# The sums' low products ahead of the others in pieces with an adding transfer, and the fourth group with two direct pieces

## The chip, the core and the metric

The kernel runs on one core of a Trainium2 chip. The metric is the device time of one execution in microseconds (us); three runs of the kernel before gave 2460.9, 2458.1 and 2459.9, with a median of 2459.9. Four engines work side by side: TensorE (PE) multiplies matrices, VectorE (DVE) and ScalarE (ACT) work on elements, GpSimd (POOL) here mostly issues transfers, and SyncE (SP) issues the loads. Each engine runs its instructions in the order in which the program issues them.

## The reference

One encoder block on 256 tokens of width 2048, all in fp32. It is framed by two gated feed-forward parts (FFN1 and FFN2), with a recurrent mixing part and a cross attention between them:

```python
def swiglu(h, w_up, w_down):
    gate, up = jnp.split(h @ w_up, 2, axis=-1)
    return (jax.nn.silu(gate) * up) @ w_down
...
x = x + 0.5 * swiglu(rms_norm(x, ffn1_norm), ffn1_w_up, ffn1_w_down)
...   # gated linear recurrence (HGRN2), RG-LRU, their merge
x = x + cross_attention(rms_norm(x, xattn_norm), rms_norm(mem, mem_norm), wq, wkv, wo)
x = x + 0.5 * swiglu(rms_norm(x, ffn2_norm), ffn2_w_up, ffn2_w_down)
return rms_norm(x, final_norm)
```

`w_up` is 2048 x 11264 and `w_down` 5632 x 2048. The change touches only the products with `w_up` in the two FFNs, how their weights are prepared, and the place of a few additions for FFN1's input.

## The kernel before, in words

**Products of two parts.** An fp32 product is made of three matmuls on a reduced format (fp32r): high x high, low x high and high x low. So each weight tile (128 x 2048, 1 MB, `raw`) is split into `h`, a copy by ACT into the reduced format, and `l = raw - h`, a subtraction on DVE (`split`, lines 117 to 121). The activations are split likewise into `xh` and `xl`. Helper `three` (line 455) issues for a list of products first the matmuls with the high part of the weights, two for each product (lines 458 and 459), and after them the matmuls with the low part, one for each (line 461). Low products therefore always come last in a piece, and PE needs `l` later than `h`.

**Groups and pieces.** Each FFN runs over 11 groups of 512 hidden columns with their gates (counted from 0 in the code, so that g = 3 is the fourth). A group has eight pieces p, one for each pair of 128-row blocks of the 2048 inputs. `ffn_order` (from line 42) writes the order of pieces out by hand, with blocks of the down product between the groups. A piece is done in one of three ways (`PRODUCTS`, lines 467 to 472; an entry names the activations' combination, the weights' combination and the accumulator):

- "plain" has 8 products, 24 matmuls, and uses the weights as they are (group 0 only).
- "fast" is a scheme of Strassen's kind with 7 products, 21 matmuls. Its first three products use parts of the weights themselves (`h` and `l`), its last four use sums of weights: `td` is made by three additions or subtractions on DVE (lines 217 to 219) and split into `th` (ACT, row L120) and `tl` (DVE, row L121), 1024 columns at a time.
- "mixed" has 8 products and 24 matmuls into the accumulators of the fast scheme. It combines activations, and needs the weights alone, no sums of them. Its weights are split as in "plain".

All matmuls of these pieces multiply a 128 x 128 activation block by a 128 x 512 part of the weights. From the fourth group on the pieces come in the order 1, 3, 4, 0, 2, 5, 6, 7, then four down blocks of 24 matmuls each; piece 0 is "mixed", the other seven "fast".

**Adding transfers.** To relieve DVE, the low part of some tiles is made without it: ACT copies the negated raw weights, rounded to the reduced format, into `l`, and a transfer issued by POOL adds the weights to it from memory. `plan_ffn` (line 130) says which tile takes which way. "fast added" (pieces 3, 4, 5 and 6 from the fourth group on) copies 1536 columns at line 224 and issues a 768 KB transfer at line 225; the copy `h` (line 226) follows. "added" (some down blocks) does it for a whole tile of 1 MB in `begin_added` (lines 190 to 197), with `h` made later at line 204. POOL's transfers go through one queue in order; the raw loads go through SP's.

**What sets the order.** `weights` (line 169) prepares tiles two pieces ahead of their use, in the order of the plan; an "added" tile's load, copy and transfer are issued one piece earlier still (line 177). The tile framework places waits and gives out buffers: three each for `raw`, for `h` and `th`, for `l`, and three shared by `td`, `tl` and the group's result `ev`; eight PSUM banks. A buffer of `l` is free again when the last matmul that reads it is done. Functions hung on a plan index (`rest`, `late_sums`, line 608) issue DVE's additions for FFN1's activation sums: for q = 1, 2, 3 at the indices 16, 17 and 18, behind the last subtraction issued.

Of the kernel before, what the change touches and what calls it, by code (L numbers as in the profile page):

```python
# [41 lines left out]
def ffn_order():  # L42

    out, down = [("plain", 0, p) for p in range(8)], [("down", 0, 1, c, 0) for c in range(4)]
    for g in range(1, NG):
        if g < 3:  # L50
            out += [(("mixed", "fast")[p % 2], g, p) for p in (0, 1, 2, 3, 5, 4, 7, 6)]
        else:
            out += [("fast" if p else "mixed", g, p) for p in (1, 3, 4, 0, 2, 5, 6, 7)]
        if g > 2 and g % 2:
            down = [("down", g - 2, 2, c, b) for c in range(4) for b in (g - 2, g - 1)]
        n = 2 if g < 3 else 4
        out, down = out + down[:n], down[n:]
    return out + [("down", NG - 2, 2, c, b) for c in range(4) for b in (NG - 2, NG - 1)]


@with_exitstack
def block_kernel(ctx: ExitStack, tc: tile.TileContext, xT, xin, memT, vec, gfin, bgate, lruw, wu1, wd1, win, wv,
# [30 lines left out]
    def bank(name="acc"):  # L93
        return psum.tile([P, 512], F32, name=name, tag="acc")
# [35 lines left out]
    def plan_ffn(name, wu, wd):  # L130
        for e in orders[name]:
            src = wd[e[4], e[3]] if e[0] == "down" else wu[e[1], e[2]]
            kind = "fast" if e[0] == "fast" else "plain"
            if e[0] == "down" and 0 < e[4] < NG - 1 and e[4] % 2 == 0 and e[3] % 2:
                kind = "added"
            if e[0] == "fast" and e[1] > 2 and e[2] in (3, 4, 5, 6):
                kind = "fast added"
            plan.append(((name,) + e, src, kind))

# [29 lines left out]
    def weights(*key):  # L169
        while plan and len(ahead) < 2:  # L170
            i = next(planned)
            k, src, kind = plan.pop(0)
            if i == 0:
                in_turn.enter_context(tc.manual_schedule(engines={sp.engine, act.engine, dve.engine}))
            if i < len(head):
                head[i]()
            if plan and plan[0][2] == "added":
                begun.append(begin_added(plan[0][1]))
            ahead.append((k, prepare(src, kind, 4 if i < 4 else 1)))
            if i in rest:  # L180
                rest[i]()
            if i == 7:
                in_turn.close()
        k, w = ahead.pop(0)
        assert k == key, (k, key)
        return w
# [79 lines left out]
    def flush(late):  # L266
        while late:
            late.pop(0)()
# [183 lines left out]

        return sums

    def three(products):

        for acc, (ah, al), (bh, bl), start, _ in products:
            pe.matmul(acc, ah, bh, start=start, stop=False)  # L458
            pe.matmul(acc, al, bh, start=False, stop=False)  # L459
        for acc, (ah, al), (bh, bl), _, stop in products:  # L460
            pe.matmul(acc, ah, bl, start=False, stop=stop)  # L461

    def part(pair, i, n):
        return [v[:, i * n:(i + 1) * n] for v in pair]
# [9 lines left out]
    def ffn(name, pairs, sq, then, begin=(), sums=()):  # L474
# [12 lines left out]
        def activate(sg, gate, up, t):  # L487

            act.activation(sg, gate, ACT.Silu, scale=rstd[:, t:t + 1])
            dve.scalar_tensor_tensor(out=sg, in0=up, scalar=rstd[:, t:t + 1], in1=sg, op0=ALU.mult, op1=ALU.mult)  # L490

        def turn(g, hid):
            for y in range(2):
                acc = bank()
                for z in range(2):
                    for t in range(2):
                        pe.transpose(acc[:, z * T + t * P:][:, :P], hid[t][:, (2 * y + z) * P:][:, :P], ident)  # L497
                o = slot(F32R, "hidop")
                ov = o.rearrange("p (z s c) -> p z s c", z=2, s=2)
                av = acc.rearrange("p (z c) -> p z c", z=2)  # L500
                act.activation(ov[:, :, 0], av, ACT.Copy)
                dve.tensor_tensor(out=ov[:, :, 1], in0=av, in1=ov[:, :, 0].bitcast(F32), op=ALU.subtract)
                hids[2 * g + y] = o
# [9 lines left out]
        for at, e in enumerate(order):  # L513
            w = weights(name, *e)
            kind = e[0]
            following = order[at + 1][0] if at + 1 < len(order) else None
            if kind != "down":
                g, p = e[1:]
                fast = kind == "fast"
                products = []  # L520
                for i, (a, b, n) in enumerate(PRODUCTS[kind]):
                    u = uses[g, n]
                    if u[0] == (p, i):
                        accs[n] = bank()
                    own, less = pairs[p]
                    products.append((accs[n], part(own, a, P) if a >= 0 else part(less, -1 - a, P), part(w[b // 4] if fast else w, b % 4, 512),
                                     u[0] == (p, i), u[-1] == (p, i)))
                three(products)
                last = at + 1 == len(order) or order[at + 1][1] != g or following == "down"
                ends = kind != "plain" and uses[g, 0][-1][0] == p  # L530
                if ends or last:
                    if ends or kind == "plain":
                        ev = scoped["wide"].tile([P, 2048], F32, name="ev", tag="wide")
                        e0, e1, e2, e3 = (ev[:, i * 512:(i + 1) * 512] for i in range(4))
                        if rstd is None:
                            with tc.issue_after(done["high"]):
                                rstd = sq.rstd_tokens()
                if ends:
                    act.activation(e0, accs[0], ACT.Copy)
                    dve.tensor_tensor(out=e1, in0=accs[5], in1=e0, op=ALU.add)  # L540
                    dve.tensor_tensor(out=e2, in0=accs[4], in1=e1, op=ALU.add)
                if last:
                    if kind == "plain":
                        activate(e0, accs[0], accs[1], 0)
                        activate(e3, accs[3], accs[2], 1)
                    else:
                        for o, n, x in ((e0, 1, e0), (e1, 3, e1), (e1, 2, e1)):
                            dve.tensor_tensor(out=o, in0=accs[n], in1=x, op=ALU.add)
                        activate(e0, e0, e1, 0)
                        for o, n, x in ((e3, 6, e2), (e2, 3, e2)):  # L550
                            dve.tensor_tensor(out=o, in0=accs[n], in1=x, op=ALU.add)
                        activate(e3, e3, e2, 1)
                    late.append((4 if g else 2, lambda g=g, hid=(e0, e3): turn(g, hid)))
            else:
                first, n, c, block = e[1:]
                if block == first:
                    accs["down"] = [bank(), bank()]
                for t in range(2):
                    products = []
                    for k in range(4):  # L560
                        a = hids[2 * block + k // 2][:, k % 2 * 512:][:, :512]
                        products.append((accs["down"][t], (a[:, t * P:][:, :P], a[:, T + t * P:][:, :P]),
                                         part(w, k, 512), block == first and k == 0, block == first + n - 1 and k == 3))
                    three(products)
                    if block == first + n - 1:
                        o = xt[c][:, t * 512:(t + 1) * 512]
                        done["residual"] = dve.scalar_tensor_tensor(out=o, in0=accs["down"][t], scalar=0.5, in1=o,
                                                                    op0=ALU.mult, op1=ALU.add).ins
                        if block == NG - 1:
                            then(c, t)  # L570
            if sums and not begin:
                sums.pop(0)()
            flush(begin)
            tick()
# [33 lines left out]
    def late_sums(q):  # L608
        with tc.issue_after(done["low"]):
            sums1[q](((0, "sums"),))  # L610

    for q, i in ((1, 16), (2, 17), (3, 18)):
        rest[i] = lambda q=q: late_sums(q)


# [49 lines left out]
    with scope(**FFN_POOLS):  # L665
        ffn("ffn1", pairs1, sq1, to_mix)
# [313 lines left out]
    for m in range(KT):  # L980
        acc = product(xs3.tiles, weights("q", m), late)
# [12 lines left out]
    for m in range(KT):  # L994
        acc = product(ms.tiles, weights("k", m))
# [53 lines left out]
    for h in range(HEADS):  # L1049
        for j in range(4):  # L1050
            acc = bank()
# [144 lines left out]
```

## Time and profile before

| | |
|---|---|
| median of three runs | 2459.9 us |
| the profiled execution's own time | 2457.71 us |
| its span | 2455.6 us |
| PE busy | 2427.0 us, 99% |
| DVE busy | 1883.5 us, 77% |
| ACT busy | 1486.4 us, 61% |
| POOL busy | 70.1 us, 3% |
| read from memory | 539.18 MB, 220 GB/s over the span |
| adding transfers of up weights | 64 of 768 KB |
| adding transfers of down weights | 16 of 1 MB |

The span is the stretch from the first to the last recorded instruction; the time of an execution has about 2 us more around it. In the profile's rows "L461 PE MATMUL acc<-l,xh" is a matmul issued at line 461, writing `acc` and reading `l` and `xh`. A number in square brackets or after the last bar is the engine's idle time just before, and the arrow names what it waited for. FFN1 lies between 0 and about 720 us, its fourth group at about 165 to 207 us; FFN2 lies between about 1750 us and the end, its fourth group at about 1900 to 1942 us.

### The profile page before, as it was taken

To read this page: it belongs to the slowest core of one execution; us is meant where nothing else is said; L and a number is where in the kernel's file an instruction comes from. 1 tells how busy PE (TensorE), PEld (TensorE's weight loads), DVE (VectorE), ACT (ScalarE), POOL (GpSimd) and SP (SyncE) were. 2 spreads that over 40 slices of the span, in tenths; PEclk is the share of its full clock that TensorE was granted. 3 is DMA by queue.
4 is the path that set the end of the run, shared out by engine and by line. 5 is a ranking of instruction groups with operands and counts; after the bars stand their busy time and mean duration, and the time that the engine had idled before them with its cause. 6 is when DMAs were issued, how large, how long until landed. Compare 5 with 4: busy or idle time off the path is not lost.

```text
span 2455.6 us, 30385 instructions
## 1 busy us (share of the span) xinstructions
PE 2427.0 (99%) x12202; PEld 2025.3 (82%) x12202; DVE 1883.5 (77%) x2057; ACT 1486.4 (61%) x1481; POOL 70.1 (3%) x84
## 2 busy tenths in 40 slices
PE   9999999999999999999999999999999999999998
PEld 8877888878788888888888888888888888887887
DVE  7998999989765757567665676556689999998985
ACT  8566677677564444477434554455555677776774
POOL 0000000000000000000000000000000000000000
PEclk9999999999999999999999999999999999999999
DMA  7578898989855544446554655444555989998894
GB/s 295 188 224 267 272 265 268 274 272 266 256 174 192 184 172 177 176 159 229 193 189 182 213 199 189 172 171 154 186 191 180 285 272 274 271 274 259 264 267 155
DMA packets 82220, 543.24 MB, mean 221 GB/s; under 512 B 9120, under 2 KB 9376, under 8 KB 24224
## 3 DMA queue, kind: packets, MB, share of 16 engines
q1 hardware_dynamic: 69840, 473.06, 52.5%
q0 software_dynamic: 11520, 67.11, 14.7%
q8 instruction: 95, 1.56, 0.2%
q10 hardware_dynamic: 720, 1.13, 0.1%
q14 instruction: 45, 0.37, 0.0%
HBM read 539.18 MB, written 2.10 MB: 220 GB/s over the span
## 4 chain that ended last, share of the span: by engine, by line
PE 88%; DMA 9%; ACT 1%; DVE 1%; issue 1%; ACTq 0%; SPq 0%; DVEq 0%
PE acc L461 16%; PE acc L458 14%; PE acc L459 14%; PE acc L240 11%; DMA l<-wu 8%; PE acc L261 8%; PE acc L262 8%; PE acc L264 8%; PE acc L244 5%; ACT l L224 1%; PE acc L497 1%; DMA raw<-wu 1%; PE acc L398 1%; ACT h L120 0%; PE acc L773 0%
## 5 line engine op out<-in xcount | busy, mean ns | idle before, releaser
L121 DVE TENSOR_TENSOR l<-raw,h 128x2048 fp32r<-128x2048 f32 (+2 forms) x372 | 790.0, 2128 | 337.0 <-ACT h L120 335.4
L120 ACT ACTIVATE h<-raw 128x2048 fp32r<-128x2048 f32 (+2 forms) x372 | 662.0, 1784 | 471.3 <-PE acc L262 205.7
L458 PE MATMUL acc<-h,xh 128*128 128x512 f32 x1256 | 490.6, 391 | 0.8 <-ACT h L120 0.8
L459 PE MATMUL acc<-h,xl 128*128 128x512 f32 x1256 | 488.9, 390 | 0.0
L120 ACT ACTIVATE h<-td 128x1024 fp32r<-128x1024 f32 x256 | 266.0, 1057 | 180.2 <-PE acc L459 88.8
L121 DVE TENSOR_TENSOR tl<-td,h 128x1024 fp32r<-128x1024 f32 x256 | 308.5, 1221 | 68.5 <-ACT h L120 66.9
L261 PE MATMUL acc<-h,ops 128*128 128x512 f32 x832 | 326.9, 393 | 0.0
L262 PE MATMUL acc<-h,ops 128*128 128x512 f32 x832 | 324.3, 390 | 0.0
L458 PEld LDWEIGHTS acc<-h,xh 128*128 128x128 f32 x1256 | 236.3, 188 | 51.7 <-ACT h L120 2.3
L240 PE MATMUL acc<-ops,h 128*128 128x512 f32 x1152 | 278.0, 393 | 0.3
L459 PEld LDWEIGHTS acc<-h,xl 128*128 128x128 f32 x1256 | 236.3, 188 | 49.0
L458 PE MATMUL acc<-h,hidop 128*128 128x512 f32 x704 | 275.7, 392 | 0.0
L459 PE MATMUL acc<-h,hidop 128*128 128x512 f32 x704 | 274.3, 390 | 0.0
L240 PEld LDWEIGHTS acc<-ops,h 128*128 128x128 f32 x1152 | 211.9, 188 | 42.9 <-DVE ops L301 0.9
L461 PE MATMUL acc<-l,xh 128*128 128x512 f32 x744 | 202.6, 394 | 17.7 <-DMA l<-wu 17.7
L264 PE MATMUL acc<-l,ops 128*128 128x512 f32 x832 | 206.1, 390 | 0.0
L461 PE MATMUL acc<-l,hidop 128*128 128x512 f32 x704 | 188.3, 389 | 0.0
L264 PEld LDWEIGHTS acc<-l,ops 128*128 128x128 f32 x832 | 156.2, 188 | 32.4
L261 PEld LDWEIGHTS acc<-h,ops 128*128 128x128 f32 x832 | 156.2, 188 | 32.3
L461 PEld LDWEIGHTS acc<-l,xh 128*128 128x128 f32 x744 | 138.2, 188 | 54.1 <-DMA l<-wu 26.7
L262 PEld LDWEIGHTS acc<-h,ops 128*128 128x128 f32 x832 | 156.3, 188 | 31.6
L217 DVE TENSOR_TENSOR td<-raw 128x1024 f32<-128x1024 f32 x128 | 155.9, 1218 | 6.1 <-DMA raw<-wu 3.9
(221 smaller groups left out, 2598.7 us busy)
## 6 DMA issues: line engine op xcount, KB each, us to landing
raw<-wu SPq DMA_DIRECT2D x172, 1024.0 KB, 6.1
raw<-wd SPq DMA_DIRECT2D x88, 1024.0 KB, 5.7
l<-wu POOLq DMA_DIRECT2D x64, 768.0 KB, 9.7
raw<-win SPq DMA_DIRECT2D x40, 1024.0 KB, 4.8
raw<-wg SPq DMA_DIRECT2D x32, 1024.0 KB, 4.8
l<-wd POOLq DMA_DIRECT2D x16, 1024.0 KB, 10.7
raw<-wab SPq DMA_DIRECT2D x16, 1024.0 KB, 4.8
raw<-wout SPq DMA_DIRECT2D x16, 1024.0 KB, 4.8
```

Of the source, the lines that this page charges most:

```text
L120: done["high"] = act.activation(h, raw, ACT.Copy).ins
L121: done["low"] = dve.tensor_tensor(out=l, in0=raw, in1=h.bitcast(F32), op=ALU.subtract).ins
L217: dve.tensor_tensor(out=two[0], in0=raw[:, None, :512].broadcast_to([P, 2, 512]), in1=two[1], op=ALU.subtract)
L224: act.activation(l[:, 512:], raw[:, 512:], ACT.Copy, scale=-1.0)
L240: pe.matmul(acc, h[:, k * P:(k + 1) * P], xs[k], start=k == 0, stop=False)
L244: done["product"] = pe.matmul(acc[:, :T], l[:, k * P:(k + 1) * P], xs[k][:, :T], start=False, stop=k == KT - 1).ins
L261: pe.matmul(accs[t], x[:, t * P:][:, :P], h[j], start=first and j == 0, stop=False)
L262: pe.matmul(accs[t], x[:, T + t * P:][:, :P], h[j], start=False, stop=False)
L264: done["product"] = pe.matmul(accs[t], x[:, t * P:][:, :P], l[j], start=False, stop=last and j == 3).ins
L458: pe.matmul(acc, ah, bh, start=start, stop=False)
L459: pe.matmul(acc, al, bh, start=False, stop=False)
L461: pe.matmul(acc, ah, bl, start=False, stop=stop)
```

## The change

It has two parts.

**The order of low products.** In fast pieces with an adding transfer, `three` now issues the low products of the sums (`tl`, products 3 to 6, four matmuls) ahead of those of the weights themselves (`l`, products 0 to 2, three matmuls). A function `adds` names these pieces: 3, 4, 5 and 6, from the fifth group on.

**The fourth group** (g = 3, in both FFNs). Its order becomes 1, 3, 0, 4, 2, 6, 5, 7. Piece 6 is "mixed" like piece 0, 24 matmuls for 21. Both mixed pieces take the way "added", a whole-tile adding transfer begun a piece earlier; the six fast pieces make `l` on DVE, so that this group has two adding transfers of 1 MB for four of 768 KB. Since piece 6 doesn't need the activation sums of the last quarter before the fifth group, the additions for q = 3 move from plan index 18 to 26.

```diff
         else:
-            out += [("fast" if p else "mixed", g, p) for p in (1, 3, 4, 0, 2, 5, 6, 7)]
+            out += [("mixed" if p == 0 or g == 3 and p == 6 else "fast", g, p)
+                    for p in ((1, 3, 0, 4, 2, 6, 5, 7) if g == 3 else (1, 3, 4, 0, 2, 5, 6, 7))]
...
+def adds(e):
+
+    return e[0] == "fast" and e[1] > 3 and e[2] in (3, 4, 5, 6)
...
-            kind = "fast" if e[0] == "fast" else "plain"
+            kind = "fast" if e[0] == "fast" else "added" if e[:2] == ("mixed", 3) else "plain"
             if e[0] == "down" and 0 < e[4] < NG - 1 and e[4] % 2 == 0 and e[3] % 2:
                 kind = "added"
-            if e[0] == "fast" and e[1] > 2 and e[2] in (3, 4, 5, 6):
+            if adds(e):
                 kind = "fast added"
...
-    def three(products):
+    def three(products, last=0):
+
 
         for acc, (ah, al), (bh, bl), start, _ in products:
             pe.matmul(acc, ah, bh, start=start, stop=False)
             pe.matmul(acc, al, bh, start=False, stop=False)
-        for acc, (ah, al), (bh, bl), _, stop in products:
+        for acc, (ah, al), (bh, bl), _, stop in products[last:] + products[:last]:
             pe.matmul(acc, ah, bl, start=False, stop=stop)
...
-                three(products)
+                three(products, 3 if adds(e) else 0)
...
-    for q, i in ((1, 16), (2, 17), (3, 18)):
+    for q, i in ((1, 16), (2, 17), (3, 26)):
         rest[i] = lambda q=q: late_sums(q)
```

## The prediction

> **What bounds the kernel now.** I read the page's busy table first, then its costliest groups, then the waits of TensorE (PE) by stretch, the order of time around single waits, and at last the chain behind one of them. The page, with columns of groups "busy, mean ns of one | idle before, releaser":
>
> ```profile
> span 2455.6 us, 30385 instructions
> ...
> PE 2427.0 (99%) x12202; PEld 2025.3 (82%) x12202; DVE 1883.5 (77%) x2057; ACT 1486.4 (61%) x1481; POOL 70.1 (3%) x84
> ...
> L461 PE MATMUL acc<-l,xh 128*128 128x512 f32 x744 | 202.6, 394 | 17.7 <-DMA l<-wu 17.7
> ```
>
> PE is the bound: busy for 99%, so only two things move the time, the number of matmuls and what PE waits for. One group carries nearly all that it waits for: line 461 is the low product with the weights' `l`, and its releaser is the adding transfer `l<-wu`. No other edit can win much. The waits of PE in four stretches (us in total, times, longest): FFN1 up to the end of its fourth group (130 to 207 us, both rows), FFN1's groups five to eleven (207 to 720), FFN2's up to its fourth group (1890 to 1942), FFN2's five to eleven (1942 to 2456):
>
> ```profile
> PE acc L461 <- DMA l<-wu: 3.5, 2, 2.7
> PE acc L458 <- ACT h L120: 0.8, 1, 0.8
> PE acc L461 <- DMA l<-wu: 7.8, 8, 2.1
> PE acc L461 <- DMA l<-wu: 0.9, 1, 0.9
> PE acc L461 <- DMA l<-wu: 5.6, 8, 1.6
> ```
>
> So 13.4 us in 16 waits fall where the first part of the change works, and 5.2 us in the two fourth groups, where the second part does. What one wait really costs, PE in order of time (start, duration, instruction, idle before):
>
> ```profile
> 258.26 0.39 PE L459 MATMUL acc<-h,xl 128*128 128x512 f32 x1
> 259.79 0.97 PE L461 MATMUL acc<-l,xh 128*128 128x512 f32 x3 [1.15 <-DMA l<-wu]
> 260.60 1.08 PE L461 MATMUL acc<-tl,xh 128*128 128x512 f32 x4
> 261.52 0.39 PE L458 MATMUL acc<-h,xh 128*128 128x512 f32 x1
> ...
> 636.46 0.75 PE L461 MATMUL acc<-l,xh 128*128 128x512 f32 x2 [2.09 <-DMA l<-wu]
> ...
> 2311.84 0.96 PE L461 MATMUL acc<-l,xh 128*128 128x512 f32 x3 [1.04 <-DMA l<-wu]
> ```
>
> Matmuls follow each other by less than a row's 0.39, which overlaps its neighbours: the undisturbed rows at 364.28 and 364.96 further down give 0.68 us from start to start for three, 0.2267 each. From 258.26 eight starts should reach 260.07; they reached 261.52. The wait cost 1.45 where the row says 1.15: 0.16 more because the matmul before it ended only in the model, 0.13 because the three `l` matmuls behind the wait ran at 0.27 each. I add 0.29 to every wait: 13.4 + 16 x 0.29 = 18.0 us are lost in the later groups.
>
> The clock, by stretch (PE, PEld, DVE, ACT and POOL busy, granted clock, DMA share, GB/s):
>
> ```profile
> 193.30:196.70 3.40, 2.92 (x7) 2.37 (x8) 2.80 (x3) 1.51 (x2) 0.00 (x0) 0.50 0.95 402
> 637.00:640.50 3.50, 3.50 (x10) 2.70 (x9) 3.00 (x2) 0.75 (x1) 0.00 (x0) 0.51 0.73 264
> 130.00:207.00 77.00, 72.70 (x314) 58.68 (x313) 69.70 (x70) 49.10 (x41) 4.50 (x5) 0.98 0.76 245
> ```
>
> Twice the clock is at 0.5 for 3.4 us, right beside the two longest waits (2.7 and 2.1 us). Each costs 3.4 x 0.5 = 1.7 us. No stretch follows a wait of 1.6 us or less.
>
> **Part one: the sums' low products first (groups five to eleven, pieces 3 to 6, both FFNs).** The four `tl` matmuls go ahead of the three `l` matmuls: no instruction is added or removed, and on ACT, DVE, POOL and SP these groups keep their order. `l` is needed 4 x 0.2267 = 0.91 us later. A wait's start delay is its idle plus 0.16; those up to 0.91 (idle up to 0.75) vanish. Eight of the sixteen are longer (the first 1.15 at 259.79, the longest 2.09 at 636.46, the last 1.04 at 2311.84; their idle adds up to 9.78). They keep 9.78 + 8 x 0.16 - 8 x 0.91 = 3.8 us and 8 x 0.13 = 1.0. Saved: 18.0 - 4.8 = **-13.1 us** (bounds: 0 if the transfers come as much later, -18.0 if they catch up).
>
> This needs the sums early. VectorE (DVE) in the stretch of that first wait:
>
> ```profile
> 253.36 2.44 DVE L121 TENSOR_TENSOR tl<-td,h 128x1024 fp32r<-128x1024 f32 x2
> ...
> 263.84 1.22 DVE L121 TENSOR_TENSOR tl<-td,h 128x1024 fp32r<-128x1024 f32 x1
> ```
>
> `tl` is done at 255.80 and PE would take it at 258.49: 2.7 us early. What is late next is the second row, the `tl` of the following piece 7, made by DVE itself: done at 265.06, read by PE at 265.82. Without the wait PE comes at most 0.9 us sooner, so this cover is just used up, and costs nothing or some hundredths; the 77% of DVE say that it can't become the bound over a group.
>
> The longest wait at 636 falls to 2.09 + 0.16 - 0.91 = 1.3 us, below the 1.6 that was never followed by half clock: **-1.7 us** (bounds 0 and -1.7). The Trainium skill, "TensorE: Matmul & The Clock Gate", section on the HAM clock gate, has the clock halve only after an idle stretch longer than a window of about 3.4 us. These rows disagree on the cause, since the waits are 2.1 and 2.7 us, and agree on the length of 3.4; by that rule both stretches would be unrelated to the waits and stay, and the sum below would be 3.4 us smaller, 2446.
>
> Against it stands that `l` is released 0.91 us later. How `l` comes about, in the chain behind the wait of another group's piece 6 (start, us, what):
>
> ```profile
> 369.65 1.83 PE acc L461 x8
> 371.48 0.02 issue
> 371.50 1.36 ACT l L224
> ...
> 373.40 11.40 DMA l<-wu
> ```
>
> ScalarE (ACT) copies the negated raw into a free buffer, POOL issues the transfer, which adds the weights in 11.4 us. The eight matmuls ahead are the low products of piece 0, whose buffer piece 6 takes. Piece 0 is "mixed" and keeps its order, so piece 6, which waits most, starts its transfer no later by this. Piece 5 takes piece 4's, at which PE and ACT show:
>
> ```profile
> 364.28 0.84 PE L461 MATMUL acc<-l,xh 128*128 128x512 f32 x3
> 364.96 1.07 PE L461 MATMUL acc<-tl,xh 128*128 128x512 f32 x4
> 365.76 1.49 ACT L224 ACTIVATE l<-raw 128x1536 fp32r<-128x1536 f32 x1 [0.17 <-DMA raw<-wu]
> ```
>
> The buffer is free at 365.12 now and would be at 366.03, the end of `tl`; the copy started at 365.76 when the raw weights landed. So it is 0.27 us later here. In the other groups the raw lands later against PE; I find 0 to 0.37, above nothing in four. I take 4 x 0.27 = **+1.0 us** (bounds 0, and 14 x 0.37 = 5.2 if POOL's queue, which runs the transfers one by one, hands it on to piece 6 in every group).
>
> **Part two: the fourth group.** Piece 6 becomes "mixed": 24 matmuls for 21. Two FFNs: 6 x 0.2267 = **+1.4 us**, on the path, certain. Four 768 KB transfers per FFN (pieces 3 to 6) become two of 1 MB, begun one piece earlier, for pieces 0 and 6. DVE's and DMA's prices (forms of all DVE groups; transfers as KB, median us to landing):
>
> ```profile
> L121 DVE TENSOR_TENSOR tl<-td,h 128x1024 fp32r<-128x1024 f32 x256 | 308.5, 1221 | 68.5 <-ACT h L120 66.9 <-PE acc L461 1.3
> L217 DVE TENSOR_TENSOR td<-raw 128x1024 f32<-128x1024 f32 x128 | 155.9, 1218 | 6.1 <-DMA raw<-wu 3.9 <-PE acc L461 1.2 <-PE acc L459 0.7
> L121 DVE TENSOR_TENSOR l<-raw,h 128x1536 fp32r<-128x1536 f32 x64 | 112.1, 1752 | 3.5 <-ACT h L120 3.5
> L219 DVE TENSOR_TENSOR td<-raw,td 128x512 f32<-128x512 f32 x128 | 88.1, 689 | 2.2
> ...
> L441 DVE TENSOR_TENSOR xs<-xg 128x128 f32<-128x128 f32 x44 | 10.8, 284 | 0.0
> ```
>
> ```profile
> l<-wd POOLq DMA_DIRECT2D x16, 1024.0 KB, 10.7
> ```
>
> A piece's sums and their split cost DVE 1.22 + 2 x 0.69 + 2 x 1.22 = 5.04 us. Before: 7 x 5.04, three subtractions of 1.75 and one of 1.75 x 4/3 = 2.3 for the mixed piece, whole = 42.8. After: 6 x (5.04 + 1.75) = 40.7, less by 2.1, against 174 x 0.2267 = 39.4 us of PE. ACT loses the four L224 copies of 1.49 and gains two whole ones; it isn't near its limit. SP's loads of the mixed pieces move ahead of their neighbours', which delays a fast piece's raw by at most one load.
>
> FFN1 lost in its fourth group 3.5 + 0.8 + 3 x 0.3 + 1.7 (half clock) = 6.9 us. The four waited-for transfers are gone, and the two new ones start a piece earlier, piece 0's with room, piece 6's with 0 to 1.5 us (10.7 us against about two and a half pieces of 4.8). But DVE at 40.7 for 39.4 stays the limit in a stretch where it was busy 69.70 of 77, and the late sums of the activations' last quarter move from the third group to just ahead of this one: four additions of 0.28 and a split of 0.69 on DVE, 1.8 us, with the first piece's `tl` only 0.5 us early. I charge 1.3 of it, let DVE-bound waits of about 1.6 stay, and take **-4.0 us** (bounds 0 and -6.9). FFN2's fourth group lost 0.9 + 0.3 = 1.2: **-0.8 us** (bounds 0 and -1.2).
>
> **Sum.** -13.1 - 1.7 + 1.0 + 1.4 - 4.0 - 0.8 = -17.2 us. The profiled execution took 2457.7 by its own time (2.1 more than its span), the median is 2459.9, 2.2 higher; the sum goes onto both: 2440.5, or 2442.7 as a median.
>
> **Rivals.**
> - Half clock doesn't hang on the waits and both stretches stay: -17.2 + 3.4 = -13.8, **2446**. For it: only two cases to go by. Against: both lie at the longest two waits.
> - The fourth group gains nothing: DVE-bound waits and the 1 MB transfer of piece 6 take the place of the old ones, the moved sums cost their whole 1.8. -13.1 - 1.7 + 1.0 + 1.4 + 1.8 = -10.6, **2449**. For it: DVE is above PE there. Against: it has 2.1 us less than before.
> - The change doesn't do what it says: transfers of piece 6 land as much later as they are needed later, by POOL's serial queue. Then only the four waits of pieces 4 and 5 go (delays of 0.70, 0.37, 0.04 and 0.55, with 0.13 each: 2.2): -2.2 + 1.4 - 4.8 = -5.6, **2454**. Against: piece 6's copy starts when piece 0's products end, not when piece 5's transfer does.
> - Slower: the later release holds ACT, which works in order, at the copy of pieces 4, 5 and 6; the copies of `th` behind it come later, DVE's `tl` and `td` behind those, and so PE. 14 groups x 3 releases x 0.6 us = 25, less 17: **2468**. It decides from 17.2 / 42 = 0.41 us handed on per release. For it: `td`, `tl` and all splits hang on ACT's turn. Against: rows show 0.27 at one of three, and DVE is idle for a fifth of the span and more.
>
> **How the numbers follow.** Forecast 0.62, half clock 0.10, fourth group 0.12, no gain at piece 6 0.10, slower 0.06. The forecast's own range, from the fourth group's bounds (+4.8 and -3.3): 2438 to 2448. The range given, 2434 to 2452, takes in the first three cases, 0.84. A measurement can tell about 0.2% (4.9 us) from no change: the first three are faster, and of the fourth, which lies on that bound, a quarter: 0.86. Same 0.08, slower 0.06.
>
> **What would show it.** PE's idle before `acc<-l,xh` of line 461 (468 after) falls from 17.7 to 2 to 4 us in about eight places (3.8 less 8 x 0.16 is 2.5, and what the fourth group keeps), and none is put before `acc<-tl,xh` in pieces 3 to 6; no stretch at 0.5 after 600 us; six more matmuls in all; waits of the fourth group move from the transfer to DVE or ACT. It is wrong if idle appears ahead of line 465's `h` or of `tl`, if the 768 KB transfers land later than 9.7 us in the median, or if piece 7 waits for its `tl` in most groups.

## The result and the profile after

The changed kernel takes 2439.15 us (median of four runs, 2437.53 to 2443.84) against 2459.75 of the kernel before: a ratio of 0.992, with a 95% interval from 0.9903 to 0.9937. Measured once more later, both on one chip, the two kernels gave 2439.44 and 2456.59, a ratio of 0.9933 (0.9918 to 0.9948). So it is faster by 17 to 21 us, 0.7 to 0.8%, which both intervals keep clear of no change; the forecast was 2443, and 17.2 us. The page of the changed kernel:

```profile
span 2438.2 us, 30368 instructions
...
PE 2422.7 (99%) x12208; PEld 2026.4 (83%) x12208; DVE 1876.3 (77%) x2051; ACT 1479.7 (61%) x1473; POOL 66.5 (3%) x80
...
L465 PE MATMUL acc<-h,xh 128*128 128x512 f32 x1254 | 489.1, 391 | 2.1 <-ACT h L126 2.1
...
L468 PE MATMUL acc<-l,xh 128*128 128x512 f32 x750 | 201.0, 391 | 3.2 <-DMA l<-wu 3.1
```

PE does six more matmuls (12208 for 12202), and its idle ahead of the `l` products falls from 17.7 to 3.2 us. What has grown stands at line 465: 2.1 us until ACT has an `h`, where the kernel before had 0.8 at line 458; 0.25 and 0.86 of it lie in FFN1's first two groups, 1.00 in FFN2's fourth. The waits in the four stretches that the prediction shows for the kernel before; FFN1's up to its fourth group has none, then FFN1's groups five to eleven, FFN2's up to its fourth group, FFN2's groups five to eleven:

```profile
PE acc L468 <- DMA l<-wu: 1.7, 4, 0.7
PE acc L465 <- ACT h L126: 1.0, 1, 1.0
PE acc L468 <- DMA l<-wu: 1.4, 3, 0.6
```

The piece that waited 1.15 us at 259.79 before, in PE's order of time after:

```profile
252.81 1.07 PE L468 MATMUL acc<-tl,xh 128*128 128x512 f32 x4
254.43 0.96 PE L468 MATMUL acc<-l,xh 128*128 128x512 f32 x3 [0.56 <-DMA l<-wu]
255.23 0.39 PE L465 MATMUL acc<-h,xh 128*128 128x512 f32 x1
```

The four `tl` products run where PE stood still; seven starts from 252.81 take 2.42 us where 7 x 0.2267 = 1.59 would do, so 0.83 is lost of the 1.45 before. There is no half clock before the very end, and through most of FFN1's fourth group PE is never idle (stretch, PE, PEld, DVE, ACT, POOL busy, clock, DMA share, GB/s):

```profile
165.00:210.00 45.00, 45.00 (x200) 37.05 (x200) 43.52 (x44) 32.88 (x26) 1.73 (x2) 1.00 0.84 264
```

Where the time went is seen by stage. The table is worked out from the trace of each run: the time between the first matmuls of two groups, in the order in which the program issues them (us; "five" and so on are groups, the columns "6-11" and "5-11" end where the last matmul of their FFN starts). By this measure FFN1's fourth group begins at 155.9 us before and at 157.2 after; the about 165 us given for it further up is too late.

| run | FFN1 1-3 | FFN1 four | FFN1 five | FFN1 6-11 | between, and FFN2 1-3 | FFN2 four | FFN2 5-11 | span |
|---|---|---|---|---|---|---|---|---|
| before | 149.1 | 69.3 | 63.7 | 424.6 | 1187.8 | 63.7 | 481.4 | 2455.6 |
| after | 150.2 | 63.2 | 62.3 | 417.4 | 1187.7 | 64.6 | 476.7 | 2438.2 |
| before again | 149.1 | 69.6 | 64.2 | 421.4 | 1187.7 | 63.6 | 481.9 | 2454.0 |
| after again | 149.0 | 63.5 | 61.7 | 419.1 | 1187.6 | 64.8 | 475.8 | 2437.2 |
| first part alone | 149.1 | 70.6 | 65.0 | 417.1 | 1187.7 | 63.0 | 477.9 | 2446.3 |
| second part alone | 149.0 | 63.2 | 62.8 | 423.0 | 1187.8 | 64.7 | 478.6 | 2445.3 |
| first part in the fourth groups too | 149.1 | 67.8 | 65.8 | 417.5 | 1187.9 | 63.3 | 476.6 | 2444.0 |
| after, sums at index 18 | 149.4 | 65.9 | 63.1 | 417.8 | 1187.8 | 64.9 | 478.6 | 2443.5 |
| after, `l` of piece 6 held | 149.0 | 63.3 | 61.8 | 417.0 | 1187.8 | 63.6 | 475.6 | 2434.1 |
| after, not piece 4 | 149.0 | 63.2 | 61.8 | 418.5 | 1187.8 | 64.8 | 475.6 | 2436.9 |
| after, memsets at the start | 148.9 | 63.4 | 62.3 | 419.7 | 1187.7 | 64.7 | 477.8 | 2440.8 |
| after, mixed pieces plain | 149.0 | 63.7 | 66.8 | 417.8 | 1187.8 | 63.3 | 478.4 | 2443.1 |

In the first pair groups five to eleven give 13.3 us (1.4 + 7.2 + 4.7), FFN1's fourth group 6.1, FFN2's loses 0.9, and FFN1's first three lose 1.1. The same code differs by up to 3 us in a column, with the transfers of the execution, so smaller differences in one row prove little.

### The profile page after: what moved, and what is told of

The parts are those of the page before. It is cut to its first block, busy times and chain, and to the rows that moved or that the text cites. A ratio compares the mean times of both kernels' runs of the same rounds, so it can differ in the third digit from the quotient of the medians.

```text
span 2438.2 us, 30368 instructions
## 1 busy us (share of the span) xinstructions
PE 2422.7 (99%) x12208; PEld 2026.4 (83%) x12208; DVE 1876.3 (77%) x2051; ACT 1479.7 (61%) x1473; POOL 66.5 (3%) x80
## 4 chain that ended last, share of the span: by engine, by line
PE 89%; DMA 6%; DVE 3%; ACT 1%; issue 1%; ACTq 0%; DVEq 0%; SPq 0%
PE acc L468 16%; PE acc L465 15%; PE acc L466 15%; PE acc L246 11%; PE acc L267 8%; PE acc L268 8%; PE acc L270 8%; PE acc L250 6%; DMA l<-wu 4%; DMA raw<-wu 1%; DVE l L127 1%; PE acc L504 1%; ACT h L126 1%; PE acc L404 1%; ACT l L230 0%
## 5 line engine op out<-in xcount | busy, mean ns | idle before, releaser
L127 DVE TENSOR_TENSOR tl<-td,h 128x1024 fp32r<-128x1024 f32 x252 | 303.6, 1221 | 70.0 <-ACT h L126 69.2
## 6 DMA issues: line engine op xcount, KB each, us to landing
l<-wd POOLq DMA_DIRECT2D x16, 1024.0 KB, 10.1
```

The costliest lines, as they stand in the source:

```text
L127: done["low"] = dve.tensor_tensor(out=l, in0=raw, in1=h.bitcast(F32), op=ALU.subtract).ins
```

## The experiments

**One part at a time.** The first kernel has the first part of the change alone (against the kernel before; `adds` begins with the fourth group here, so that its transfers stay):

```diff
-                three(products)
+                three(products, 3 if adds(e) and e[1] > 3 else 0)
```

> The first part of the change alone: sums' low products first in groups five to eleven, the fourth group and the late sums as before. Theory: PE's waits for the adding transfer in these groups are cut by 0.91 us each and nothing else moves, so it gains what the changed kernel gained there, 8.7 us in FFN1 and 4.7 us in FFN2: 13.4 us against the kernel before, about 2446 on the median, with the fourth groups' waits (3.5 and 0.8 us, 0.9 us) and the half clock at 193 us as they were. Rival: part of the gain in the later groups came from the fourth group handing on fewer late buffers; then groups five and six of FFN1 gain less than in the changed kernel and the whole is under 11.

2448.4 us against 2456.7 on the same chip, 8.3 less, ratio 0.9963 (0.9949 to 0.9977). The rival's sign is there: group five takes 65.0 us, more than before. PE's wait there, and DVE behind it:

```profile
241.41 0.73 PE L468 MATMUL acc<-tl,xh 128*128 128x512 f32 x2 [1.70 <-DVE tl L127]
```

```profile
239.00 1.23 DVE L223 TENSOR_TENSOR td<-raw 128x1024 f32<-128x1024 f32 x1 [3.31 <-DMA raw<-wu]
```

The `tl` that PE waits for is piece 4's, and DVE, in order, made it late because it first stood 3.31 us until the raw weights of piece 2 landed, for the difference that comes ahead of it. In the kernel before, DVE waited for the same weights, but with both halves of piece 4's `tl` already made:

```profile
233.26 2.44 DVE L121 TENSOR_TENSOR tl<-td,h 128x1024 fp32r<-128x1024 f32 x2
236.67 1.23 DVE L217 TENSOR_TENSOR td<-raw 128x1024 f32<-128x1024 f32 x1 [0.97 <-DMA raw<-wu]
```

So the built program runs DVE in another order, although the edit names only matmuls: put side by side by names and shapes, ACT, POOL and SP keep their order between the two traces, and on DVE one instruction moves in each of the 14 groups, the first difference of piece 2, to ahead of the second half of piece 4's `tl`. The changed kernel has the same new order and yet no wait here. SP's loads show why, first in this kernel, then in the changed one (start, us):

```profile
224.31 0.33 SPq L217 DMA_DIRECT2D raw<-wu  x1
229.11 5.83 SPq L220 DMA_DIRECT2D raw<-wu  x2
```

```profile
212.44 0.33 SPq L217 DMA_DIRECT2D raw<-wu  x1
221.30 16.11 SPq L220 DMA_DIRECT2D raw<-wu  x4
```

Line 217 loads piece 0 of group five, and the first load of line 220 behind it piece 2. With the old fourth group piece 2's is issued at 229.1, 2.7 us behind the group's first matmul (226.4), and DVE has it 12.6 us behind; with the new one it is issued at 221.3, 0.9 us behind (220.4), and DVE doesn't wait for it. Piece 0's went out 2 us ahead of that matmul in the one and 8 us in the other. The kernel before loads as late as this one (227.91, also 2.7 us behind), so it takes both, the new order on DVE and the late load, to make PE wait.

The second part alone (against the changed kernel, as are the edits below unless said otherwise):

```diff
-                three(products, 3 if adds(e) else 0)
+                three(products)
```

> The second part alone: the new fourth group and the moved sums, low products in the old order everywhere. Theory: FFN1's fourth group gains 6.2 us as in the changed kernel, FFN2's loses 0.9, the rest stays as before with its 13.4 us of waits in 16 places and the half clock at the 2.1 us wait: -5.3 us, about 2454. Rival: with the fourth group repaired PE comes earlier to group five and waits there instead, and the gain is under 3 us.

2447.62 us, 9.1 less, ratio 0.9961 (0.9947 to 0.9976). The fourth groups came as expected (63.2 and 64.7), group five is shorter, not longer (62.8). The rival falls. All its waits for `l`, which lie in the later groups, sum to less than the 13.4 us in 16 places that the first trace of before had there:

```profile
PE acc L468 <- DMA l<-wu: 10.4, 14, 1.5
```

FFN2's groups five to eleven have the same instructions as before and took 478.6 us where before took 481.4 and 481.9; some 3 of the 9.1 us thus come with no change of code there, and what remains, against the trace "before again", is near 6.4 us in FFN1's fourth group and 1.4 in group five, less 1.1 in FFN2's fourth. The two parts together, 8.3 + 9.1 = 17.4, come to the whole change; with those 3 us unexplained, the close fit is in part luck.

**The order of the sums in the fourth groups too**, which otherwise stay as they were (against the kernel before; `adds` begins with the fourth group):

```diff
-                three(products)
+                three(products, 3 if adds(e) else 0)
```

> Sums' low products first in the fourth groups too, which otherwise stay as before (seven fast pieces, four transfers). Theory: it shortens the fourth group's waits by 0.91 us each: of 6.9 us lost in FFN1's, 2 x 0.91 and the half clock of 1.7 go when the longest wait falls from 2.7 to 1.8, so -3.5 there and -1.2 in FFN2's, -18 in all, about 2442: the second part of the change is then worth only 1 to 3 us more than this. Rival: the wait goes over to tl, since DVE is the limit of that stretch; then FFN1's fourth group gains less than 1 us and the whole is about -15.

2446.58 us, 10.1 less, ratio 0.996 (0.9945 to 0.9975), short of the theory's 18 and of the rival's 15. FFN1's fourth group gains 1.5 to 1.8 us, neither 3.5 nor under 1, and group five loses 1.5 to 2.0 of it again, to a wait of 2.4 us for DVE's `tl`. In the fourth group itself the wait for piece 6's transfer is 3.3 us where before had 2.7 and 3.0, although `l` is needed later. So the reorder does nothing for these two groups together while the fourth has four transfers: there it needed the second part. FFN2's fourth group gains 0.3 to 0.5.

**The sums at their old place:**

```diff
-    for q, i in ((1, 16), (2, 17), (3, 26)):
+    for q, i in ((1, 16), (2, 17), (3, 18)):
```

> The changed kernel with the last quarter's sums left at plan index 18. The prediction charged 1.3 us for their new place. In the changed kernel's trace they run at 142.6 to 146.9 us, where DVE waits for PE before the group's result. Theory now: the move costs nothing, so this kernel is within 0.5 us of the changed one in FFN1's groups two to four, or slower by up to 1.8 us if the sums at the old place delay the third group's tiles. Rival (the prediction's charge): this kernel is 1.3 us faster there.

2441.68 us against 2456.7, ratio 0.994 (0.9925 to 0.9955), 15.0 less where the whole change gives 17.1 to 20.6. FFN1's fourth group is 2.4 to 2.8 us longer than in the changed kernel, the three before 0.4, group five 0.8 to 1.4: more than the 1.8 allowed, and against the prediction's charge. The profiled execution was the slowest of the four, 3.6 us above their median, so the trace overstates it; by the medians the old place costs the whole kernel some 2 us. DVE at the end of the third group, here and then in the changed kernel:

```profile
141.00 1.21 DVE L127 TENSOR_TENSOR tl<-td,h 128x1024 fp32r<-128x1024 f32 x1
143.69 0.69 DVE L547 TENSOR_TENSOR ev<-acc,ev 128x512 f32<-128x512 f32 x1 [1.48 <-PE acc L468]
...
148.99 1.41 DVE L497 SCALAR_TENSOR_TENSOR ev<-ev,rtok 128x512 f32<-128x512 f32 x2 [0.90 <-ACT ev L496]
150.32 2.28 DVE L127 TENSOR_TENSOR l<-raw,h 128x2048 fp32r<-128x2048 f32 x1
```

```profile
142.03 0.69 DVE L547 TENSOR_TENSOR ev<-acc,ev 128x512 f32<-128x512 f32 x1
142.63 0.28 DVE L447 TENSOR_TENSOR xs<-xg 128x128 f32<-128x128 f32 x1
142.83 0.69 DVE L548 TENSOR_TENSOR ev<-acc,ev 128x512 f32<-128x512 f32 x1
143.43 0.28 DVE L447 TENSOR_TENSOR xs<-xs,xg 128x128 f32<-128x128 f32 x1
143.63 0.29 DVE L447 TENSOR_TENSOR xs<-xg 128x128 f32<-128x128 f32 x1
143.83 0.28 DVE L447 TENSOR_TENSOR xs<-xg,xs 128x128 f32<-128x128 f32 x1
144.03 2.29 DVE L127 TENSOR_TENSOR l<-raw,h 128x2048 fp32r<-128x2048 f32 x1
```

At the old place DVE stands 1.48 us until PE ends the group, 0.90 more for ACT, and only then splits the next down block. With the move the last sums run among the first additions of the result, a split of 2.29 us comes ahead of the rest, and DVE has no idle there. It enters the fourth group some 2 us further on.

**Both kernels again, on one chip.**

> The kernel before itself, unchanged, with a profile beside the next runs. The two parts alone gave 8.3 and 9.1 us where 13.4 and 5.3 were expected. Theory: the loss in groups five to eleven hangs on how fast the adding transfers land, which differs from execution to execution: over a floor of 477.2 us in FFN1 and 473.8 in FFN2 (the shortest seen, 61.5 a group) the first trace of before lost 11.1 and 7.6 us, the kernel with the second part alone, which has the same code there, 8.6 and 4.8. Then this trace also lies between 12 and 19 in sum. Rival: the new fourth group hands a better state to the later groups; then this one loses 18 or more again and the second part is worth 5 us beyond its own group.

> The changed kernel unchanged, on the same chip as the kernel before with its own profile. Theory: -17 to -20 us by the medians, with 3 to 7 us over the floor in groups five to eleven of both FFNs, and the fourth groups at 63.2 and 64.6 us as in the first trace; the 1.1 us that its group two lost in the first trace to a raw load of 7.5 us is gone, as it lies ahead of anything that the change moves. Rival: that loss comes from the change and is there again.

2456.12 and 2439.44 us: 17 less. Before loses 8.4 and 8.1 us over the floor, 16.5 in all, within the theory's band and short of the rival's 18. After loses 3.6 and 2.0. This speaks against the rival, but doesn't settle FFN2: there before lost 7.6 and 8.1 us in its two traces and the second part alone 4.8 in its one, and whether those 3 us come from the new fourth group or from the execution stays open. The 1.1 us of FFN1's first three groups are gone (149.0), so they belong to one execution's load: that trace has a raw load of 7.5 us at 75.6, and PE waits 0.86 behind it.

**Longer waits, and the clock.** A kernel in which POOL writes a scratch tile ahead of the transfer:

```diff
+            for _ in range(held.pop(0)):
+                nc.gpsimd.memset(scratch, 0.0)
             nc.gpsimd.dma_start(l[:, 512:], src[:, 512:], accum_op=ALU.add)
```

> The changed kernel with POOL held up by memsets of a scratch tile (4 for each unit) ahead of the adding transfer of piece 6: 0, 0, 1, 0, 2, 0, 3 units in FFN1's groups five to eleven and 0, 0, 4, 0, 5, 0, 6 in FFN2's. It makes waits of several lengths with nothing else changed. The clock's changes in all traces lie on a grid of 3.413 us. Theory: half clock follows a stretch of that grid in which PE stood still for more than about 2.0 us (1.94 was not followed, 2.15 was), so a wait of 2.2 to 3.9 us halves the clock only where the grid doesn't divide it, and a longer one always. First rival (the prediction): a wait above 2.0 us halves it always. Second rival (the rule of a whole idle stretch of 3.4 us): no wait under 3.4 us does.

It settles nothing, because the edit didn't do what was meant. Nothing in the program ties the memsets to a transfer, and in the built kernel all 84 run at the very start, between 0.7 and 27.0 us:

```profile
L234 POOL MEMSET scratch<- 128x192 f32 x84 | 21.7, 258 | 5.1 <-POOLq L1194 0.3
```

On the other engines every instruction has its place of the changed kernel. PE's waits for `l` are 4.1 us, the longest 1.0, and the clock doesn't halve before the end. So this is a third trace of the changed kernel, and shows how far they differ: over the floor of groups five to eleven it loses 8.8 us, the other two 5.4 and 5.6. For the question of the clock the copy itself is repeated:

```diff
-            act.activation(l[:, 512:], raw[:, 512:], ACT.Copy, scale=-1.0)
+            for _ in range(1 + again.pop(0)):
+                act.activation(l[:, 512:], raw[:, 512:], ACT.Copy, scale=-1.0)
```

> The changed kernel in which ACT makes the negated copy for piece 6 two, three or four times in some groups, each 1.41 us from start to start: 0, 1, 0, 2, 0, 2, 0 more in FFN1's groups five to eleven and 1, 0, 2, 0, 3, 0, 1 in FFN2's. It asks what the memsets could not, since they ran while POOL was idle anyway. Theory: PE waits about 1.5 us where one copy is added, 3 us for two, 4.5 us for three; the clock is at 0.5 for 3.41 us after each stretch of its grid of 3.413 us in which PE stood still for 2.15 us or more, and after none with 1.94 or less; so after all or nearly all of the waits of 4 us and more, some of those of 3, and none of 1.5. First rival: every wait over 2.0 us halves it, however it lies in the grid. Second rival: only waits over 3.4 us do.

From start to start, one copy more makes PE late by 0.3 and 1.6 us or not at all, two more by 3.8 to 4.8, three by 6.0; less than the theory said for one in most places, more for the others. (FFN1's group five was late by 1.3 without an added copy.) Stretches of the clock's grid in this kernel, by the columns above:

```profile
314.59:318.00 3.41, 2.01 (x9) 1.39 (x8) 3.41 (x5) 2.46 (x3) 0.00 (x0) 1.00 0.70 285
318.00:321.42 3.42, 3.42 (x16) 2.77 (x16) 3.05 (x2) 2.06 (x2) 0.00 (x0) 1.00 0.80 261
440.88:444.29 3.41, 0.08 (x1) 0.00 (x0) 3.41 (x5) 1.52 (x1) 0.00 (x0) 1.00 0.87 177
444.29:447.70 3.41, 2.87 (x7) 2.29 (x8) 1.34 (x1) 0.00 (x0) 0.00 (x0) 0.50 0.95 308
2253.36:2256.77 3.41, 1.54 (x7) 0.94 (x5) 3.41 (x4) 3.27 (x3) 0.00 (x0) 1.00 1.04 259
2256.77:2260.18 3.41, 0.00 (x0) 0.00 (x0) 3.28 (x2) 0.00 (x0) 0.00 (x0) 1.00 1.01 255
2260.18:2263.59 3.41, 2.85 (x7) 2.27 (x8) 0.00 (x0) 0.00 (x0) 0.00 (x0) 0.50 1.02 430
```

All four waits of 3.8 us and more halve the clock, two of them for two stretches (6.83 us from 574.00 and from 2127.06); none of 1.6 us or less does. Taken alone this leaves both rivals standing. The kernel with the sums first everywhere tells more: its wait of 3.3 us lay over two stretches, and its 2.4 us for `tl` in one:

```profile
189.05:192.46 3.41, 1.95 (x9) 1.09 (x7) 1.76 (x3) 0.59 (x1) 0.00 (x0) 1.00 1.03 280
192.46:195.87 3.41, 1.60 (x7) 1.34 (x8) 2.16 (x3) 2.79 (x3) 0.00 (x0) 1.00 1.00 396
195.87:199.29 3.42, 3.42 (x17) 2.83 (x16) 3.42 (x4) 3.20 (x2) 0.00 (x0) 1.00 0.33 137
236.84:240.25 3.41, 1.06 (x5) 0.65 (x4) 3.14 (x3) 2.18 (x2) 0.00 (x0) 1.00 0.48 202
240.25:243.66 3.41, 3.41 (x9) 2.67 (x9) 3.41 (x3) 1.86 (x2) 0.29 (x1) 0.50 0.25 41
```

The longer wait left 1.95 and 1.60 us of work in either stretch, and the clock stayed; the shorter left 1.06 in one, and it halved. The first rival falls here, the second at every wait of 2.0 to 2.7 us that halved it.

**Piece 4 in the old order:**

```diff
-                three(products, 3 if adds(e) else 0)
+                three(products, 3 if adds(e) and e[2] != 4 else 0)
```

> The changed kernel with piece 4 in the old order, so that its l buffer, which piece 5 takes, is free 0.91 us sooner. The prediction charged 1.0 us in sum for that release. Theory: piece 5's copy comes earlier by up to 0.5 us in the groups where the raw weights were there, piece 5 has that much more to spare and piece 6's transfer, behind it in the queue, lands earlier by at most that; piece 4 itself was only just in time in a few groups of the kernel before and waits there again (0.4 to 0.7 us in two or three places). So within 1.5 us of the changed kernel. Rival: the queue hands the whole on, and piece 6's 2 to 3 us of waits go: 2 to 4 us faster than the changed kernel.

2438.68 us against 2456.65, ratio 0.9927 (0.9912 to 0.9941); the changed kernel's 0.9933 lies in that interval. A wait of 0.56 us is back at a piece 4 in one group, and piece 6 still waits in two, 2.0 us in all (seven with 3.1 and five with 2.5 in the two traces of the changed kernel). The rival's 2 to 4 us aren't there; a gain of some tenths can't be told.

**The fourth group's mixed pieces without adding transfers:**

```diff
-            kind = "fast" if e[0] == "fast" else "added" if e[:2] == ("mixed", 3) else "plain"
+            kind = "fast" if e[0] == "fast" else "plain"
```

> The changed kernel with the two mixed pieces of the fourth group split by DVE, without adding transfers. Theory: DVE is the limit of that group, and two subtractions of 2.29 us more take it from 40.7 to 45.3 us for 39.4 of PE: FFN1's fourth group is 3 to 5 us longer than the changed kernel's 63.2 to 63.5, or hands that on to group five, FFN2's 1 to 4 us longer than 64.7. Rival: what freed the group is the end of the four waited-for transfers, not DVE's load; then it is within 1 us.

2446.1 us against 2456.65, 10.6 less where the changed kernel has 17, ratio 0.9956 (0.9942 to 0.9971). The group itself is as short (63.7), and group five pays, 66.8 us for 61.7 to 62.3, at one place:

```profile
237.55 0.73 PE L468 MATMUL acc<-tl,xh 128*128 128x512 f32 x2 [3.39 <-DVE tl L127]
```

Half clock follows it for 3.4 us. It is again piece 4's `tl`, behind a raw load of piece 2 that is issued 3.4 us after the group's first matmul and for which DVE stands 3.33 us. In FFN2 the fourth group is 1.3 to 1.5 us shorter than with the transfers, where the theory had it longer, and group five takes 63.7 for 61.7 to 61.8, so that the two groups together differ by 0.6. So the two transfers are needed in FFN1, and what they save falls due one group later; in FFN2 they bring next to nothing.

**A further step.** Piece 6's `l` products behind the high products of piece 7, and FFN2's fourth group as before with the sums first:

```diff
...
+        now, later = products[last:] + products[:last], []
+        if hold:
+            now, later = products[last:], products[:last]
-        for acc, (ah, al), (bh, bl), _, stop in products[last:] + products[:last]:
+        for acc, (ah, al), (bh, bl), _, stop in held + now:
             pe.matmul(acc, ah, bl, start=False, stop=stop)
+        held[:] = later
...
```

> The changed kernel with two more steps: piece 6's three l products are issued only behind the high products of piece 7 (3.2 us later still), and FFN2's fourth group is as before, with the sums first. Theory: PE's waits for piece 6's transfer (3.1 us idle in 7 places in the changed kernel's trace, 5 with what stands behind each) go, and FFN2's fourth group loses 1.3 us less: 4 to 6 us faster than the changed kernel, about 23 below the kernel before. Rival: the l buffer comes free 3.4 us later, which the down blocks behind piece 7 need; their split on DVE comes late and PE waits there for l or h, up to 2 us in each of 14 groups, and it is slower than the changed kernel.

2437.9 us, 1.5 less than the changed kernel on the same chip, ratio 0.9928 (0.9912 to 0.9945) against 0.9933: not told apart by the runs (2435.93 to 2438.58 against 2438.12 to 2440.43), and not the 4 to 6 us of the theory. The profiled span is 3.1 us shorter, but that execution was the fastest of its four. What PE still waits for outside the start:

```profile
PE acc L466 <- ACT h L126: 0.8, 2, 0.5
```

No wait for a transfer is left, and the rival's waits at the down blocks don't come. But each of the later groups takes 61.75 us where the shortest in other runs are 61.5: PE loses about 0.3 at the last high products of piece 7, which need a `th` that ACT ends just too late.

## Why the prediction was right, and where it wasn't

The sum was right, and the time fell 4 us under the forecast, within the given range. (The forecast's own range, 2442.7 with +4.8 and -3.3, is 2439.4 to 2447.5 and not 2438 to 2448; the median lies just below it.) By spans the change is worth 17.4 and 16.8 us, forecast 17.2; the rest of the first pair's 20.6 lies in how the profiled executions stand to their medians, 2.0 below before and 0.8 above after. That it fits to a few tenths is in part luck: the reorder alone brought less than forecast, FFN1's fourth group more.

- **Waits of groups five to eleven.** Forecast 13.1 + 1.7 - 1.0 = 13.8 us; measured 13.3 and 10.9 for both parts together. The mechanism was right: shortened waits remained in 7 places with 3.1 us where some eight with 2.5 were forecast. But the forecast gave it all to the reorder, which was too much: alone this brought 7.5 us there (against before again), and added to the second part about 8. In FFN1's group five alone it lost 0.8: DVE's late `tl` of piece 4 took the place of the waits for `l`. Here the sentence that "on ACT, DVE, POOL and SP these groups keep their order" failed: on DVE the first difference of piece 2 moved ahead of that `tl`. And the step that said what is late next looked at pieces 6 and 7 of that group, where `tl` had room, and not at the pieces ahead of them. The rest of the shortfall is not traced.
- **Half clock.** It went, but in before again there is none after 600 us either, the end apart, so the 1.7 us belong to one execution; they are in the 13.3 and not in the 10.9. The rule behind it was wrong: what counts isn't the length of a wait, but how much of it falls into one stretch of a fixed grid.
- **The later release, +1.0.** Nothing speaks against it: taking it away in piece 4 changed less than the runs can tell. That also means that the size isn't shown.
- **FFN1's fourth group.** Forecast -4.0 + 0.7 = -3.3, measured -6.1 both times. Two charges were wrong, 1.3 us for the moved sums and 1.6 for waits on DVE. The sums' new place is worth 2.4 us in that group by the trace with the old place, some 2 us by the medians, where a cost had been charged. The forecast had taken DVE's idle ahead of the group's result for no reserve.
- **FFN2's fourth group.** Forecast -0.1, measured +0.9 and +1.2. PE waits 1.0 us for ACT's `th` of piece 3, which ACT takes up only when the raw weights of piece 4, the next fast piece, have landed and their `h` is made (ACT, changed kernel):

```profile
1895.86 1.49 ACT L126 ACTIVATE h<-raw 128x1536 fp32r<-128x1536 f32 x1 [2.09 <-DMA raw<-wu]
1897.25 1.03 ACT L126 ACTIVATE h<-td 128x1024 fp32r<-128x1024 f32 x1
```

  The sentence that a load moved ahead "delays a fast piece's raw by at most one load" was there, and was given no price. That the loads moved ahead make this one late, and not the adding transfer of 1 MB that runs beside it, isn't shown: the kernel with plain mixed pieces has neither, and no such wait.
- **The signs of being wrong.** Two of the three came up, though the sum held. Idle appeared ahead of line 465's `h`, 2.1 us in the first trace, and ahead of `tl` at one piece 4 in the second (0.24). The 768 KB transfers landed after 10.0 and 9.8 us in the median, where 9.7 was the bound. Neither was large enough to undo the gain.
- **The rivals.** Half clock didn't stay, FFN1's fourth group did gain, piece 6's transfers didn't move with the need, and nothing came out slower. Where the buffers' late release was feared, waits for `l` went.

## What to carry to other kernels

When an operand arrives late, let the products that don't need it run first; it adds no instruction, and is worth each wait up to the length of what is moved ahead, less what becomes late elsewhere. Before such a gain is counted, compare the built order of every engine, which can move without an edit to it, and ask what is late next in every piece of the group where it goes: here a `tl` behind a raw load, which the change to the group ahead had to bring forward. An instruction moved into an in-order queue is priced by the hole that it falls into, so look for the queue's own waits at the new place first.

## What the runs showed that was not expected

The clock's changes lie on a grid of 3.413 us that runs through the whole execution: in the first trace of before the two half-clock stretches begin at 193.31 and 637.04, 443.73 apart, 130.0 times 3.413, and in each of the 13 traces all changes lie whole multiples of it apart. The kernel with the first part alone has two stretches near the bound, each with the half clock behind it:

```profile
172.18:175.59 3.41, 1.55 (x8) 0.95 (x7) 1.09 (x1) 2.29 (x2) 0.00 (x0) 1.00 1.02 423
175.59:179.01 3.42, 3.42 (x10) 2.65 (x9) 3.42 (x4) 2.04 (x2) 0.00 (x0) 0.50 0.22 91
192.66:196.07 3.41, 1.35 (x6) 1.14 (x7) 2.16 (x4) 2.55 (x3) 0.00 (x0) 1.00 0.99 378
196.07:199.49 3.42, 3.42 (x10) 2.65 (x9) 3.42 (x5) 1.91 (x1) 0.00 (x0) 0.50 0.61 208
```

Over all traces a stretch at full clock in which PE was busy for 1.35 us or less was followed by half clock, and none with 1.60 or more; at 1.55 it was, in the first row here, and at 1.54 it wasn't, at 2253 us above. The Trainium skill, "TensorE: Matmul & The Clock Gate", Part 1, has this free-running window with the same length, and there every trace agrees. Its rule that the clock halves after an idle window is too narrow here: a window 60% idle was enough. And what counts is the window and not the wait, since a wait of 3.3 us over two windows cost no clock at all.
